# Output projection, first SwiGLU strips and down projection re-staged in a hybrid decoder layer (one core)

## The chip, the cores and the metric

The kernel runs on one core of a Trainium2 chip. The metric is device time in microseconds of one execution; lower is better. The core has five engines with instruction queues of their own: TensorE (PE in the rows; PEld is its weight load), VectorE (DVE), ScalarE (ACT), GpSimd (POOL) and SyncE (SP), which here issues the DMAs. Each engine takes its instructions strictly in order, so an instruction that waits holds up everything behind it on that engine.

## The reference, cut to what matters

One decoder layer on x of 1024 tokens by 1024 channels, in fp32. Three branches (gated linear attention, forgetting attention, cross-attention) are merged with gates; the change begins behind that:

```python
x = x + merged @ w_out[l]
h2 = _rmsnorm(x, g_ffn[l])          # x * rsqrt(mean(x*x)) * g
x = x + (jax.nn.silu(h2 @ w_ffn_gate[l]) * (h2 @ w_ffn_up[l])) @ w_ffn_down[l]
```

The hidden width of the SwiGLU is 2816.

## The kernel before

Channels lie on partitions, tokens in the free dimension: x1[j][h] is one 128x512 tile, channel block j (0 to 7) of token half h (0 or 1). Every fp32 matmul is done as three matmuls of rounded parts (mm3, L843, L845, L847: hi·hi, hi·lo, lo·hi). So each operand is split first: ScalarE casts it to the rounded high part (L903, tiles h or ...h), VectorE subtracts that from the raw tile to get the low part (L904, tiles l or ...l). A weight strip comes by DMA into a raw tile w4 (128x1024) and gives one h4 and one l4.

- **Merge** (to about 924 us of the span): the branches are summed into acc and split into mgh and mgl.
- **Output projection** (out_half, L919 to L932): for token half 0 and then 1, eight products of 24 matmuls, one per channel block j: load x (L919) and the weight strip wout (L921), split, multiply, add x to the result (L927), store the sum x_d (L928), square it (L930) and add the squares (L932).
- **Norm factors** (half_factors, L940 to L947): the squares are summed over partitions on TensorE, the inverse root comes from GpSimd (L108), and a product with a diagonal (L946) spreads it to all partitions as rbc (L947). The norm weight and the factor are then applied together in one VectorE instruction (L952, normed).
- **SwiGLU** (gate_up): 11 pairs of a gate strip and an up strip, 256 hidden channels each. A strip needs seven products of a Strassen-like scheme on sums of the token and channel halves (right operands B11, B21, T2, T1, T3, B22, T4; only B11 and B21 come from token half 0 alone). A product is 12 matmuls (four blocks of 128 channels by three), so a strip is seven products and a pair fourteen. What a product leaves in PSUM is kept by a ScalarE copy (L1031, tile t) or added to a kept tile by VectorE (L994). One PSUM bank goes on accumulating after its copy, so TensorE waits for that copy. The pair ends by storing act_d (L1073); then four loads of down weights go into cells d (L1076), are summed on VectorE and stored as sum_d (L1082).
- **Down projection** (down): four blocks of 3, 3, 3 and 2 pairs, which load act_d and sum_d back, split them and add into acc, in block 0 on top of the loaded x_d (L1136).

Tiles come from rotating pools: w4 has 5 buffers, h4 and l4 3 each, the cells (x1, acc, t, T, d) 16. TensorE's order is that of the program text. The order on the other engines and on SP is set at build time by a scheduler, which lets an instruction go ahead of others when the scheduler's own estimate says that its inputs are ready.

Of the kernel before, what the change touches and what calls it, by code (L numbers as in the profile page):

```python
# [12 lines left out]
F32 = mybir.dt.float32  # L13
# [64 lines left out]
def trunk(tc, xT, memT, wT, wmkv, wmq0, wmq1, wgv, wfox, a2, par, cst, wbr, wout, wfg, wfu, wfd, outT):  # L78
# [18 lines left out]
    identr = cp.tile([P, P], F32R, name="identr")  # L97
    negr = cp.tile([P, P], F32R, name="negr")
    mhalf = cp.tile([P, 1], F32, name="mhalf")
    hbg = cp.tile([P, 24], F32, name="hbg")  # L100
    gs = cp.tile([P, 6], F32, name="gs")
    rc = cp.tile([P, KT], F32, name="rc")
    rbc = cp.tile([P, S], F32, name="rbc")
# [26 lines left out]
    psA = pool(A, "psA", space=PSUM)  # L130
    bank = lambda tag, bufs: psA.tile([P, 512], F32, tag=tag, bufs=bufs, name=tag)
# [725 lines left out]
    cell = lambda name: ap_.tile([P, 512], F32, tag="cell", bufs=16, name=name)  # L857
# [5 lines left out]
    tp = pool(BM, "tg")  # L863
# [25 lines left out]
    merge_lane()  # L889
    Y.close()  # L890

# [4 lines left out]
    w4 = lambda: ws.tile([P, S], F32, tag="w4", bufs=5, name="w4")  # L896
# [3 lines left out]
    l2 = lambda: ws.tile([P, 512], F32R, tag="l2", bufs=2, name="l2")  # L900

# [9 lines left out]
    hops = {}  # L911

    def out_half(h):
# [3 lines left out]
        for j in range(KT):  # L917
            x1[j][h] = x = cell("x1")
            nc.sync.dma_start(x, xT[j][:, sl])  # L919
            raw = w4()  # L920
            nc.sync.dma_start(raw, wout[j])  # L921
            hi, lo = split(h4(), l4(), raw)
# [4 lines left out]
            nc.vector.tensor_tensor(x, x, ps, ALU.add)  # L927
# [3 lines left out]
            if j:  # L931
                nc.vector.tensor_tensor(ssq, ssq, sq, ALU.add)  # L932
            yield ssq

    def half_factors(h, ssq):
# [11 lines left out]
        nc.scalar.copy(rbc[:, H2[h]], ps)  # L947
        yield

    def normed(k, h):  # L950
        x = x1[k][h]
        nc.vector.scalar_tensor_tensor(x, x, pr[:, C_GFFN + k:C_GFFN + k + 1], rbc[:, H2[h]], ALU.mult, ALU.mult)  # L952
        return x
# [18 lines left out]

# [5 lines left out]
    def products(A, B, nk, reads):  # L978

        banks = {}  # L980
        for i, (bk, an, bn) in enumerate(SEQ):
            first = bk not in banks
            if first:
                banks[bk] = bank8()
            ps = banks[bk]
            for k in range(nk):
                (ah, al), (bh, bl) = A(an, k), B(bn, k)
                mm3([ps], ah, al, [(bh, bl)], first and k == 0, k == nk - 1, not first)
            reads[i](ps)
            yield  # L990

    BM.close()
    hp2 = pool(root, "h2b")
    add = lambda o, a, b: nc.vector.tensor_tensor(o, a, b, ALU.add)  # L994
    sub = lambda o, a, b: nc.vector.tensor_tensor(o, a, b, ALU.subtract)

    def weights(src):
# [6 lines left out]
        a = split(h4(), l4(), ra)  # L1004
# [18 lines left out]
    def gate_up(p):  # L1023

        g = [[None, None], [None, None]]
        u = [[None, None], [None, None]]

        def keep(t, i, l):
# [5 lines left out]
        def plus(t, i, l, then):  # L1034
# [5 lines left out]
        silu = lambda i, l: nc.scalar.activation(g[i][l], g[i][l], AF.Silu)  # L1040

        def silu_last(ps):
            g[1][0] = cell("t")
            nc.scalar.activation(g[1][0], ps, AF.Silu)

        mul = lambda i, l: nc.vector.tensor_tensor(u[i][l], u[i][l], g[i][l], ALU.mult)

        def mul_last(ps):
            u[1][0] = cell("t")
            nc.vector.tensor_tensor(u[1][0], ps, g[1][0], ALU.mult)  # L1050

        reads = lambda t, then, last: [keep(t, 0, 0), plus(t, 0, 0, then), keep(t, 0, 1), keep(t, 1, 1),
                                       plus(t, 1, 1, then), plus(t, 0, 1, then), last]
        wg = weights(wfg[p])
        gg_ = products(wg, hB, 4, reads(g, silu, silu_last))
        if p == 0:
            yield from (next(gg_) for i in range(2))
        else:
            yield from gg_
        wu = weights(wfu[p])  # L1060
        uu_ = products(wu, hB, 4, reads(u, mul, mul_last))
        if p == 0:
            yield from (next(uu_) for i in range(2))
            yield from gg_
        yield from uu_
        (b11, b12), (b21, b22) = u
        t1, t2, t3, t4 = (cell("T") for i in range(4))
        sub(t1, b12, b11)
        sub(t2, b22, t1)
        sub(t3, b22, b12)  # L1070
        sub(t4, b21, t2)
        for i, t in enumerate((b11, b21, t2, t1, t3, b22, t4)):
            nc.sync.dma_start(act_d[p][i], t)  # L1073
        a11, a12, a22, a21 = d = [cell("d") for i in range(4)]
# [8 lines left out]
        yield  # L1083

    run = gate_up(0)
    next(run)
    next(fac)
    next(run)
    next(run)
# [155 lines left out]
```

## Time and profile before

| | |
|---|---|
| median of 3 runs | 1755.86 us (1755.05 to 1757.85) |
| profiled execution | 1756.35 us, of which the span from first to last instruction is 1754.6 |
| TensorE busy | 1665.9 us (95%), mean granted clock 0.985 |
| VectorE, ScalarE, GpSimd busy | 989.3 (56%), 628.9 (36%), 103.1 us (6%) |
| DMA | 219.74 MB, 125 GB/s over the span |

A row of the timeline gives the start and the duration in us, the engine, the line in the kernel, the operation and its tiles, and in square brackets how long the engine stood idle before and what released it. "x4" is four instructions in a row. Clock is the share of TensorE's full rate (2.4 GHz) that was granted; half of it is 1.2 GHz.

### The profile page before, as it was taken

How to read it: one execution, taken by the hardware profiler on the slowest of the kernel's cores; microseconds unless marked ns; L12 is line 12 of the kernel's file. 1: busy time of each engine (PE TensorE's matmuls, PEld its weight loads, DVE VectorE, ACT ScalarE, POOL GpSimd, SP SyncE). 2: the span in 40 equal slices, each digit the busy share in tenths (PEclk: the TensorE clock that was granted, in tenths of full speed). 3: DMA queues.
4: the chain of work that ended last, by engine and by line, in shares of the span. 5: the costliest groups of instructions: out<-in, count | busy, mean ns of one | idle time of the engine just before them, and what ended most of it. 6: DMA issues, size and time to landing. Idle time of an engine off the chain costs nothing.

```text
span 1754.6 us, 21924 instructions
## 1 busy us (share of the span) xinstructions
PE 1665.9 (95%) x8411; PEld 1393.1 (79%) x8411; DVE 989.3 (56%) x1577; ACT 628.9 (36%) x1072; POOL 103.1 (6%) x88
## 2 busy tenths in 40 slices
PE   8999999999999999999998968999999999699999
PEld 6889988879799999988886856777777777577777
DVE  8435553452436555454474677565566665666766
ACT  6334553232224444342122324333332333433431
POOL 2000100000010100000450000000000000000000
PEclk9999999999999999999998988999999999899999
DMA  6431221111222211236555312454444445865654
GB/s 228 133 122 58 64 73 50 61 66 58 67 72 88 62 62 34 69 116 205 191 181 198 114 48 86 150 159 155 142 142 148 148 138 165 293 209 161 197 154 141
DMA packets 152297, 219.74 MB, mean 125 GB/s; under 512 B 11120, under 2 KB 93568, under 8 KB 152192
## 3 DMA queue, kind: packets, MB, share of 16 engines
q1 hardware_dynamic: 152192, 218.34, 38.3%
q8 instruction: 66, 1.08, 0.3%
q14 instruction: 39, 0.32, 0.1%
HBM read 159.25 MB, written 59.05 MB: 124 GB/s over the span
## 4 chain that ended last, share of the span: by engine, by line
PE 75%; DVE 9%; DMA 9%; SPq 3%; issue 2%; ACT 2%; POOL 0%; DVEq 0%; ACTq 0%
PE ps L843 11%; PE ps L845 11%; PE ps L847 11%; PE pt L156 4%; PE pt L158 4%; PE pt L157 4%; PE pm L235 4%; PE pm L236 4%; PE pm L237 4%; DMA d<-in_wfd 4%; PE pm L198 2%; DMA w<-act_d 2%; DVE l L904 2%; PE pm L202 2%; PE pm L200 2%
## 5 line engine op out<-in xcount | busy, mean ns | idle before, releaser
L843 PE MATMUL ps<-hbh,h 128*128 128x512 f32 x660 | 265.7, 403 | 66.3 <-ACT t L1031 35.2
L903 ACT CAST h<-w 128x1024 fp32r<-128x1024 f32 (+4 forms) x168 | 144.6, 861 | 368.5 <-PE ps L845 296.6
L845 PE MATMUL ps<-hbl,h 128*128 128x512 f32 x660 | 262.4, 398 | 0.0
L847 PE MATMUL ps<-hbh,l 128*128 128x512 f32 x660 | 262.3, 397 | 0.0
L904 DVE TENSOR_TENSOR l<-w,h 128x1024 fp32r<-128x1024 f32 (+4 forms) x168 | 166.0, 989 | 92.5 <-ACT h L903 92.4
L843 PEld LDWEIGHTS ps<-hbh,h 128*128 128x128 f32 x660 | 124.9, 189 | 108.3 <-ACT t L1031 39.8
L235 PE MATMUL pm<-whi,hh 128*128 128x384 f32 (+2 forms) x512 | 162.2, 317 | 0.0
L237 PE MATMUL pm<-whi,hl 128*128 128x384 f32 (+2 forms) x512 | 159.0, 310 | 0.0
L236 PE MATMUL pm<-wlo,hh 128*128 128x384 f32 (+2 forms) x512 | 158.9, 310 | 0.0
L847 PEld LDWEIGHTS ps<-hbh,l 128*128 128x128 f32 x660 | 124.8, 189 | 30.3
L845 PEld LDWEIGHTS ps<-hbl,h 128*128 128x128 f32 x660 | 125.0, 189 | 28.6
L156 PE MATMUL pt<-hh,whi 128*128 128x512 f32 x352 | 142.2, 404 | 0.0
L158 PE MATMUL pt<-hh,wlo 128*128 128x512 f32 x352 | 138.1, 392 | 0.0
L157 PE MATMUL pt<-hl,whi 128*128 128x512 f32 x352 | 138.1, 392 | 0.0
L994 DVE TENSOR_TENSOR acc<-ps,acc 128x512 f32<-128x512 f32 x112 | 76.8, 689 | 50.3 <-PE ps L847 47.6
L843 PE MATMUL ps<-hah,h 128*128 128x512 f32 x264 | 103.7, 393 | 0.9 <-ACT h L903 0.9
L847 PE MATMUL ps<-hah,l 128*128 128x512 f32 x264 | 103.2, 391 | 0.9 <-DVE l L904 0.8
L845 PE MATMUL ps<-hal,h 128*128 128x512 f32 x264 | 103.0, 390 | 0.0
L235 PEld LDWEIGHTS pm<-whi,hh 128*128 128x128 f32 x512 | 96.4, 188 | 2.6
L236 PEld LDWEIGHTS pm<-wlo,hh 128*128 128x128 f32 x512 | 96.4, 188 | 2.5
L237 PEld LDWEIGHTS pm<-whi,hl 128*128 128x128 f32 x512 | 96.3, 188 | 0.0
L188 DVE TENSOR_TENSOR wlo<-raw,whi 128x512 fp32r<-128x512 f32 (+2 forms) x64 | 48.3, 756 | 77.3 <-ACT whi L187 76.8
(301 smaller groups left out, 3065.5 us busy)
## 6 DMA issues: line engine op xcount, KB each, us to landing
w<-act_d SPq DMA_DIRECT2D x33, 512.0 KB, 4.1
tg<-tg_d SPq DMA_DIRECT2D x24, 512.0 KB, 3.5
raw<-in_wT SPq DMA_DIRECT2D x22, 512.0 KB, 4.1
tg_d<-gz SPq DMA_DIRECT2D x22, 512.0 KB, 2.9
w<-in_wfg SPq DMA_DIRECT2D x22, 512.0 KB, 4.4
w<-in_wfu SPq DMA_DIRECT2D x22, 512.0 KB, 3.7
act_d<-T SPq DMA_DIRECT2D x44, 256.0 KB, 6.0
d<-in_wfd SPq DMA_DIRECT2D x44, 256.0 KB, 6.2
```

Source lines behind the costliest of these rows:

```text
L156: nc.tensor.matmul(ps, hi[:, ks], hh[k][:, sl], start=k == 0, stop=False)
L157: nc.tensor.matmul(ps, hi[:, ks], hl[k][:, sl], start=False, stop=False)
L158: nc.tensor.matmul(ps, lo[:, ks], hh[k][:, sl], start=False, stop=k == KT - 1)
L235: nc.tensor.matmul(ps[:, :n], hh[k][:, ms], hi, start=k == 0, stop=False)
L236: nc.tensor.matmul(ps[:, :n], hh[k][:, ms], lo, start=False, stop=False)
L237: nc.tensor.matmul(ps[:, :n], hl[k][:, ms], hi, start=False, stop=k == KT - 1)
L843: nc.tensor.matmul(ps, hi, a, start=first, stop=False, skip_group_check=more)
L845: nc.tensor.matmul(ps, hi, b, start=False, stop=False, skip_group_check=more)
L847: nc.tensor.matmul(ps, lo, a, start=False, stop=last, skip_group_check=more)
L903: nc.scalar.copy(hi, raw)
L904: nc.vector.tensor_tensor(lo, raw, hi.bitcast(F32), ALU.subtract)
L994: add = lambda o, a, b: nc.vector.tensor_tensor(o, a, b, ALU.add)
```

## The change

- The first wout strip (j = 0 of half 0) is loaded and split under the branches, into buffers of its own (wout0).
- rbc, identr and three other constants move to pools that are freed; cells grow from 16 to 18, w4 from 5 to 6.
- In half 1 the norm weight is applied by ScalarE (L992 of the kernel after) as soon as a block is done, ahead of the factor, which is multiplied later; for blocks 4 to 7 the block j - 4 is subtracted as well. The factor for half 1 then is a plain VectorE product.
- The first strips wfg[0], wfu[0] and wfg[1] do their first two products (B11, B21: token half 0) before the factors of half 1 are needed; the raw first halves of the latter two strips are loaded early (early, e1, e2), their other parts are made later (lazy).
- The order of the sums behind the factor changes (T2 first), and the products of q0 and q1 alternate.
- down_sums uses w4 tiles in place of cells, and stands ahead of the products of its pair instead of behind them (pair 0's stands in pair 4).
- Down block 0 no longer loads x_d into acc: its first product of each tile is copied by ScalarE. x_d is added in block 1. The loads of the next block's act_d are called at jj = 2 of the block before.

```diff
-    rbc = cp.tile([P, S], F32, name="rbc")
-    cell = lambda name: ap_.tile([P, 512], F32, tag="cell", bufs=16, name=name)
+    cell = lambda name: ap_.tile([P, 512], F32, tag="cell", bufs=18, name=name)
     merge_lane()
+    wout0 = load_split(w0p, wout[0], S, "w0", 1, 1)
     Y.close()
-    w4 = lambda: ws.tile([P, S], F32, tag="w4", bufs=5, name="w4")
+    w4 = lambda: ws.tile([P, S], F32, tag="w4", bufs=6, name="w4")
...
-            raw = w4()
-            nc.sync.dma_start(raw, wout[j])
-            hi, lo = split(h4(), l4(), raw)
+            if h == j == 0:
+                hi, lo = wout0
+            else:
+                raw = w4()
+                nc.sync.dma_start(raw, wout[j])
+                hi, lo = split(h4(), l4(), raw)
...
-    halves = [out_half(h) for h in range(2)]
-    for ssq in halves[0]:
-        pass
-    fac = half_factors(0, ssq)
-    for j, ssq in enumerate(halves[1]):
-        if j in (0, 1):
+    fac = half_factors(ssq)
+    for j, ssq in enumerate(out_half(1)):
+        if j == 0:
             next(fac)
         if j == 1:
+            rb = next(fac)
             for k in range(KT):
-                hops["B11" if k < 4 else "B21", k % 4] = hop(hp1, "ha", 8, normed(k, 0))
-    fac = half_factors(1, ssq)
+                x = x1[k][0]
+                nc.vector.scalar_tensor_tensor(x, x, gain(k), rb, ALU.mult, ALU.mult)
+                hops["B11" if k < 4 else "B21", k % 4] = hop(hp1, "ha", 8, x)
+        x = x1[j][1]
+        nc.scalar.activation(x, x, AF.Copy, scale=gain(j))
+        if j > 3:
+            sub(x, x, x1[j - 4][1])
+    fac = half_factors(ssq)
...
-        a11, a12, a22, a21 = d = [cell("d") for i in range(4)]
+    def down_sums(p):
+
+        ta, tb = w4(), w4()
+        a11, a12, a22, a21 = d = [t[:, s] for t in (ta, tb) for s in H2]
...
+    wg0 = strips(wfg[0])
+    e1, e2 = early(wfu[0]), early(wfg[1])
+    q0, q1, q2 = pairs[0].gate(wg0), pairs[0].up(late("u0", wfu[0], e1)), pairs[1].gate(late("g1", wfg[1], e2))
+    go(q0, 4)
     next(fac)
-    next(run)
-    next(run)
-    next(fac)
+    go(q0, 4)
+    go(q1, 2)
+    rb = next(fac)
+    go(q1, 6)
+    go(q2, 8)
...
     for k in range(4):
-        (b11, b12), (b21, b22) = x1[k], x1[k + 4]
-        normed(k, 1)
-        normed(k + 4, 1)
-        t2 = w4()[:, :512]
-        sub(b11, b12, b11)
-        sub(t2, b22, b11)
+        t3, t2 = x1[k + 4][1], w4()[:, :512]
+        mul(t3, t3, rb)
+        add(t2, t3, x1[k][0])
         hops["T2", k] = hop(hp2, "hb", 20, t2)
-        sub(b21, b21, t2)
+        sub(x1[k + 4][0], x1[k + 4][0], t2)
+    lazy["u0"] = strips(wfu[0], e1)
...
+    for i in range(5):
+        go(q0, 4)
+        go(q1, 4)
+    pairs[0].store(0)
+    lazy["g1"] = strips(wfg[1], e2)
     for p in range(1, NP):
-        for _ in gate_up(p):
-            pass
+        q = q2 if p == 1 else Pair.gate(pair := Pair(), strips(wfg[p]))
+        if p == 1:
+            pair = pairs[1]
+        down_sums(p)
+        if p == 4:
+            down_sums(0)
+        go(q)
+        go(pair.up(strips(wfu[p])))
+        pair.store(p)
...
-            if p0 == 0:
-                for j in (jj, jj + 4):
-                    for h in range(2):
-                        acc[j][h] = cell("acc")
-                        nc.sync.dma_start(acc[j][h], x_d[j][h])
+            if jj == 2 and not last:
+                down_ops(p0 + n)
...
+                    if acc[j][h] is None:
+                        acc[j][h] = cell("acc")
+                        nc.scalar.copy(acc[j][h], ps)
+                        return
...
+            if b == 1:
+                for j in (j1, j2):
+                    x = w4()
+                    for h, s in enumerate(H2):
+                        nc.sync.dma_start(x[:, s], x_d[j][h])
+                        add(acc[j][h], acc[j][h], x[:, s])
```

Three places show what the scheduler made of it. **First place: half 1 of the output projection.** SP's queue before, around the load of the wout strip for block j = 2 (w4_8831):

```order
L928 DMA x_d3_0_8290<-x1_8435 128x512
L921 DMA w4_8793<-in_wout 128x1024
L928 DMA x_d4_0_8292<-x1_8473 128x512
L921 DMA w4_8831<-in_wout 128x1024
L928 DMA x_d5_0_8294<-x1_8511 128x512
L921 DMA w4_8869<-in_wout 128x1024
```

SP's queue after, around the same load (now w4_8770):

```order
L941 DMA x_d5_0_8308<-x1_8523 128x512
L941 DMA x_d6_0_8310<-x1_8561 128x512
L941 DMA x_d7_0_8312<-x1_8599 128x512
L941 DMA x_d0_1_8299<-x1_8638 128x512
L941 DMA x_d1_1_8301<-x1_8685 128x512
L934 DMA w4_8770<-in_wout 128x1024
L934 DMA w4_8809<-in_wout 128x1024
```

Before, that load stood five stores ahead of the store of block 1 of half 1; after, it stands behind it. On VectorE before, the low part of that strip (l4_8834) and the first two of the eight instructions that apply weight and factor to half 0:

```order
L927 TENSOR_TENSOR x1_8672<-x1_8672,ps_8680 128x512
L904 TENSOR_TENSOR l4_8834<-w4_8831,h4_8833 128x1024
L932 TENSOR_TENSOR ssq_8625<-ssq_8625,sq_8707 128x512
L952 SCALAR_TENSOR_TENSOR x1_8323<-x1_8323,pr_97,rbc_106 128x512
L952 SCALAR_TENSOR_TENSOR x1_8359<-x1_8359,pr_97,rbc_106 128x512
```

On VectorE after, the last three of those eight and the same low part (l4_8773):

```order
L989 SCALAR_TENSOR_TENSOR x1_8523<-x1_8523,pr_97,w4_8725 128x512
L989 SCALAR_TENSOR_TENSOR x1_8561<-x1_8561,pr_97,w4_8725 128x512
L989 SCALAR_TENSOR_TENSOR x1_8599<-x1_8599,pr_97,w4_8725 128x512
L913 TENSOR_TENSOR hal_8729<-x1_8337,hah_8728 128x512
L913 TENSOR_TENSOR hal_8734<-x1_8371,hah_8733 128x512
L913 TENSOR_TENSOR l4_8773<-w4_8770,h4_8772 128x1024
```

The low part has moved from ahead of all eight to behind them and two splits.

**Second place: a pair of the SwiGLU.** ScalarE before, from the last cast of a strip on (h2 and h4 are parts of the strips to come, t the kept products):

```order
L903 CAST h2_10396<-w4_10375 128x512
L903 CAST h4_10380<-w4_10374 128x1024
L1031 COPY t_10286<-ps_10273 128x512
L1040 ACTIVATE t_10286<-t_10286 128x512
L1031 COPY t_10315<-ps_10273 128x512
L903 CAST h4_10386<-w4_10376 128x1024
```

ScalarE after, at the same place:

```order
L912 CAST h2_10432<-w4_10411 128x512
L1054 COPY t_10322<-ps_10309 128x512
L912 CAST h4_10416<-w4_10410 128x1024
L1073 ACTIVATE t_10322<-t_10322 128x512
L1054 COPY t_10351<-ps_10309 128x512
L912 CAST h4_10422<-w4_10412 128x1024
```

The first kept copy (t) of the strip now stands ahead of the cast of the next strip's first part. SP's queue after holds, in one pair, the loads of down weights, the sums' stores and the next up strip in this order:

```order
L1098 DMA w4_9998<-in_wfd 128x4x128 x2
L1098 DMA w4_9999<-in_wfd 128x4x128 x2
L1022 DMA w4_10113<-in_wfu 128x1024
L1104 DMA sum_d3_8328<-w4_9999 128x4x128 x2
L1104 DMA sum_d3_8328<-w4_9998 128x4x128 x2
L1023 DMA w4_10114<-in_wfu 128x1024
```

Before, the sums lay in cells, and no load of a strip stood behind the wait of their stores in this way.

**Third place: behind the factor of half 1.** VectorE before, where the low part of the second piece of strip wfu[0] (l4_9065) stands among the first sums of the token halves:

```order
L952 SCALAR_TENSOR_TENSOR x1_8943<-x1_8943,pr_97,rbc_106 128x512
L995 TENSOR_TENSOR x1_8323<-x1_8626,x1_8323 128x512
L995 TENSOR_TENSOR x1_8359<-x1_8672,x1_8359 128x512
L904 TENSOR_TENSOR l4_9065<-w4_9054,h4_9064 128x1024
L995 TENSOR_TENSOR x1_8397<-x1_8753,x1_8397 128x512
```

VectorE after, where that piece (w4_9187) is made and split (l4_9194) behind the low parts of nearly all the token sums (hbl, 20 of them in all):

```order
L913 TENSOR_TENSOR hbl_9268<-x1_8485,hbh_9267 128x512
L913 TENSOR_TENSOR hbl_9272<-x1_8523,hbh_9271 128x512
L913 TENSOR_TENSOR hbl_9276<-x1_8561,hbh_9275 128x512
L908 TENSOR_TENSOR w4_9187<-w4_9187,w4_9185 128x512
L913 TENSOR_TENSOR hbl_9280<-x1_8599,hbh_9279 128x512
L908 TENSOR_TENSOR w4_9188<-w4_9185,w4_9187 128x512
L913 TENSOR_TENSOR l4_9194<-w4_9187,h4_9193 128x1024
```

It has moved from the head of the stretch to its end.

## Rows read from the trace of the kernel before

**Rows 1.** The page: busy time of TensorE; granted clock in 40 slices, in tenths.

```profile
PE 1665.9 (95%) x8411; PEld 1393.1 (79%) x8411; DVE 989.3 (56%) x1577; ACT 628.9 (36%) x1072; POOL 103.1 (6%) x88
PEclk9999999999999999999998988999999999899999
```

**Rows 2.** Waits of TensorE: line, releaser, us in total, times, longest.

```profile
PE ps L843 <- ACT t L1031: 35.2, 11, 21.3
PE ps L843 <- DVE acc L994: 21.6, 9, 14.1
PE ps L843 <- DVE t L994: 8.9, 10, 1.6
```

**Rows 3.** Timeline from merge to output projection (SP, ACT, DVE, PE).

```profile
923.32 3.12 SPq L921 DMA_DIRECT2D w<-in_wout  x5
929.43 1.04 ACT L903 CAST h<-w 128x1024 fp32r<-128x1024 f32 x1 [3.13 <-DMA w<-in_wout]
930.50 1.23 DVE L904 TENSOR_TENSOR l<-w,h 128x1024 fp32r<-128x1024 f32 x1 [3.10 <-ACT h L903]
930.52 0.79 PE L843 MATMUL ps<-mgh,h 128*128 128x512 f32 x1 [6.79 <-ACT h L903]
936.64 0.42 PE L845 MATMUL ps<-mgl,h 128*128 128x512 f32 x1
```

**Rows 4.** Windows: us, TensorE busy (matmuls), granted clock, DMA share, GB/s.

```profile
1061.39:1067.00 5.61, 5.61 (x14) 0.55 0.01 3
1527.67:1533.00 5.33, 5.33 (x17) 0.73 1.07 384
```

**Rows 5.** Timeline of half 1 of the output projection, behind block 1.

```profile
990.70 0.69 DVE L927 TENSOR_TENSOR x<-x,ps 128x512 f32<-128x512 f32 x1 [2.79 <-PE ps L847]
991.41 0.33 SPq L928 DMA_DIRECT2D x_d<-x  x1
993.33 5.39 DVE L952 SCALAR_TENSOR_TENSOR x<-x,pr,rbc 128x512 f32<-128x512 f32 x8
```

**Rows 6.** DMA issues: count, KB each, median us from issue to landing.

```profile
w<-in_wfu SPq DMA_DIRECT2D x22, 512.0 KB, 3.7
d<-in_wfd SPq DMA_DIRECT2D x44, 256.0 KB, 6.2
sum_d<-d SPq DMA_DIRECT2D x44, 256.0 KB, 2.6
w<-in_wout SPq DMA_DIRECT2D x16, 512.0 KB, 4.5
```

**Rows 7.** Timeline from the output projection to pair 0 (DVE, PE).

```profile
1025.15 0.69 DVE L927 TENSOR_TENSOR x<-x,ps 128x512 f32<-128x512 f32 x1 [1.59 <-PE ps L847]
1061.39 0.79 PE L843 MATMUL ps<-hbh,h 128*128 128x512 f32 x1 [21.25 <-ACT t L1031]
1066.55 0.39 PE L843 MATMUL ps<-hbh,h 128*128 128x512 f32 x1
1086.15 0.40 PE L843 MATMUL ps<-hbh,h 128*128 128x512 f32 x1
```

**Rows 8.** Timeline of one gate strip in the pairs (ACT, PE, DVE).

```profile
1097.18 1.04 ACT L903 CAST h<-w 128x1024 fp32r<-128x1024 f32 x1 [4.85 <-PE ps L845]
1098.13 0.58 ACT L1031 COPY t<-ps 128x512 f32<-128x512 f32 x1
1098.77 0.50 PE L843 MATMUL ps<-hbh,h 128*128 128x512 f32 x1 [1.39 <-ACT t L1031]
1105.30 0.69 DVE L994 TENSOR_TENSOR d<-d 128x512 f32<-128x512 f32 x1 [3.80 <-DMA d<-in_wfd]
1111.04 0.50 PE L843 MATMUL ps<-hbh,h 128*128 128x512 f32 x1 [0.81 <-DVE t L994]
```

**Rows 9.** Timeline at the start of the down projection (DVE, PE).

```profile
1526.22 0.69 DVE L994 TENSOR_TENSOR d<-d 128x512 f32<-128x512 f32 x1 [4.98 <-DMA d<-in_wfd]
1527.67 0.76 PE L843 MATMUL ps<-hbh,h 128*128 128x512 f32 x1 [14.14 <-DVE acc L994]
```

More of the change, by code (lines that the diff above doesn't have):

```diff
@@ L911, in trunk @@
     hops = {}
+    gain = lambda k: pr[:, C_GFFN + k:C_GFFN + k + 1]
     def out_half(h):
@@ L1003, in weights @@
         s2, s1, s3, s4 = sa[:, lo_], sa[:, hi_], sb[:, lo_], sb[:, hi_]
-        a = split(h4(), l4(), ra)
+        a = first or split(h4(), l4(), ra)
         add(s1, rb_[:, lo_], rb_[:, hi_])
@@ L1054, in gate_up @@
[L1054 to L1073, printed above, removed]
-        a11, a12, a22, a21 = d = [cell("d") for i in range(4)]
+        def reads(self, t, then, last):
+            return [self.keep(t, 0, 0), self.plus(t, 0, 0, then), self.keep(t, 0, 1), self.keep(t, 1, 1),
+                    self.plus(t, 1, 1, then), self.plus(t, 0, 1, then), last]
@@ new lines, in gate, with last, up @@
+        def gate(self, w):
+            g = self.g
+            def last(ps):
+                g[1][0] = cell("t")
+                nc.scalar.activation(g[1][0], ps, AF.Silu)
+            return products(w, hB, 4, self.reads(g, lambda i, l: nc.scalar.activation(g[i][l], g[i][l], AF.Silu), last))
+        def up(self, w):
+            g, u = self.g, self.u
+            def last(ps):
+                u[1][0] = cell("t")
+                mul(u[1][0], ps, g[1][0])
+            return products(w, hB, 4, self.reads(u, lambda i, l: mul(u[i][l], u[i][l], g[i][l]), last))
@@ new lines, in store @@
+        def store(self, p):
+            (b11, b12), (b21, b22) = self.u
+            t1, t2, t3, t4 = (cell("T") for i in range(4))
+            sub(t1, b12, b11)
+            sub(t2, b22, t1)
+            sub(t3, b22, b12)
+            sub(t4, b21, t2)
+            for i, t in enumerate((b11, b21, t2, t1, t3, b22, t4)):
+                nc.sync.dma_start(act_d[p][i], t)
+    def down_sums(p):
+        ta, tb = w4(), w4()
+        a11, a12, a22, a21 = d = [t[:, s] for t in (ta, tb) for s in H2]
@@ L1137, in down @@
+    def down(b, p0, n):
+        first, last = b == 0, p0 + n == NP
+        for q in range(n):
+            if (ORDER[0], p0 + q) not in ops:
+                down_ops(p0 + q)
+        for jj in range(4):
+            if jj == 2 and not last:
+                down_ops(p0 + n)
             three = lambda t: t[:, :n * 2 * P].rearrange("p (n c) -> p n c", c=2 * P)
@@ L1167, in down @@
                      into(j1, 1, True), into(j2, 0, True)]
-            for _ in products(get, lambda name, k: ops[name, k], n, reads):
-                pass
+            if b == 1:
[4 more added lines that the diff above has]
+                        add(acc[j][h], acc[j][h], x[:, s])
+            go(products(get, lambda name, k: ops[name, p0 + k], n, reads))
     p0 = 0
-    for n in DOWN:
-        down(p0, n, p0 + n == NP)
+    for b, n in enumerate(DOWN):
+        down(b, p0, n)
         p0 += n
```

122 lines of the change are left out of this document (67 added, 55 removed).

## The prediction

> **What bounds the kernel now.** I read the page's busy shares first, then TensorE's waits, then the timeline around each of them. TensorE is busy 95% of the span and at full clock in nearly all slices [rows 1]. So little can be won but its idle time, and since its products are the same before and after, the change is worth what it takes away or adds in gaps and in half-rate matmuls (1.2 GHz granted instead of 2.4) behind gaps. Behind the merge the waits fall into five places [rows 2, 3]: 6.79 us for the first output weight strip; 21.25 us ahead of the first T2 product; ten gaps of about 1.4 us for a ScalarE copy and ten of 0.6 to 1.6 us for a VectorE addition, one of each in every later pair; 14.14 us at the start of the down projection; and 7.5 us in eight further waits of the down projection (21.6 less 14.1). A full-rate product of 12 matmuls takes 2.80 us: seven of them lie between 1066.55 and 1086.15 [rows 7]. The profiled execution took 1756.35 us, 0.5 above the median of the three runs; I work from it and take off the 0.5 at the end.
>
> **1. First output strip: -8.3.** Before, SP issues the wout loads at 923.32, the cast of the first runs at 929.43, and TensorE idles from 923.73 to 930.52 [rows 3]. It then runs at half rate: 14 matmuls start between 930.52 and 936.64, in 6.12 us where 14 x 0.233 = 3.27 would do, a loss of 2.85. After, strip 0 is split long before, and 24 matmuls (5.6 us) run from about 923.7 to 929.3. Strip 1 is then the late one: released by the same merge, it can be issued no earlier than 923.32, so its cast ends where the first cast ended, at 930.5. That leaves a gap of 1.2 to 1.8. So 6.79 + 2.85 - 1.3 = 8.3 goes. The load and split of strip 0 lie under the branches, where TensorE does not wait for them; its cover there is one cast and one subtraction of 1.04 and 1.23 us, which is the worst that it costs.
>
> **2. A new wait in half 1 of the output projection: +11.** Before, the wout strip of block 2 is loaded well ahead. After, its load is behind the store of block 1, which waits for that block's product. Call the end of that product X (990.70 before) [rows 5]. The store is issued at X + 0.71, the load behind it at about X + 1.0; it lands 4.5 later [rows 6] at X + 5.5, and its cast ends at X + 6.6. VectorE is late too: the eight scale instructions start at X + 2.6 and take 5.39 [rows 5], two splits of about 0.67 follow, and only then the low part, 1.23, which ends near X + 10.3. TensorE has the spread of the factor to do until about X + 0.9 (half of the 2.2 that both factor products take, below), then waits to X + 6.6, does the two matmuls that need no low part, and waits to X + 10.3: 5.7 + 2.8 = 8.5 idle. Half rate behind it costs about what it did behind the 6.79 (2.5 to 2.85). The gap is hidden only if the load were issued a product earlier, which the order does not allow. Lower bound: without VectorE's part 5.7 and no loss of clock, +6; upper: landing as the slowest load of the rows [rows 6], 6.2 in place of 4.5, +13. I take +11, the step by step value. The other things that half 1 gets (eight gain instructions on ScalarE of the length of a copy, four subtractions, two early splits) lie beside products of 5.6 us each and cost nothing unless ScalarE falls behind; each gain waits for a store, but what stands behind it is needed one product later.
>
> **3. Transition to the pairs: -3.** From the last addition of the output projection (1025.15) to the end of the twelfth product it takes 61.0 us before [rows 7]: four products on half 0, the 21.25 us in which VectorE scales and sums the tokens, then eight products, the first at half rate (clock 0.55 in that window [rows 4]). After, six products come first, so TensorE is free at 19.0: six of 2.80 and 2.2 for the factor's own products (before, the 15.0 us from 1025.15 to 1040.14, where the idle time begins, held four products and those, so they are under 3.8). VectorE begins its sums at about 10 and comes to the first low part of T2 behind 8 products, 4 sums and 10 other instructions of about 0.67 (14.5): T2 of q0 can go at 24.5, a gap of 5.6. T2 of q1 needs the second piece of wfu[0], whose subtraction stands behind some 23 token sums and splits: 24.5 + 23 x 0.68 gives about 40, its cast 1.04 and low part 1.23 about 42.6, a second gap of 13. Half rate behind it, then the remaining products: twelve are done at about 58. So -3. Bounds: the second gap no longer than the first, -10; the two together as long as the old one and 4 longer for a second half-rate stretch, +4.
>
> **4. Ten pairs: -20.** The ScalarE gap: a cast that had waited 4.85 us for TensorE stands ahead of the kept copy, so the copy starts 0.95 late and TensorE 1.39 [rows 8]. After, the copy stands first: 13.9 us of the 35.2 [rows 2] go. The VectorE gap: VectorE sits 3.80 us on a load of down weights, and the addition that TensorE needs comes late by 0.81 [rows 8]. After, those loads are issued a strip ahead of their sums (19.6 us, seven products) so they have landed. But the next up strip's second load is now behind the sums' stores, and the sum of that strip stands on VectorE ahead of an addition that TensorE needs. I get it issued about 5 us into the up strip, landed (3.7 [rows 6]) at 9, and the addition of the fifth product (ends at 14.0) on time with some 1.3 us to spare before TensorE needs it at 16.8. I keep 2.8 us of the 22.8 for pairs in which that margin fails, as in pair 4 with two sets of sums. Bounds: nothing left, -22.8; both VectorE waits late like the old one, -5.
>
> The Trainium skill, "DMA: Bandwidth & Descriptors", Anatomy of one DMA, prices a DMA at 2.0 us and its bytes over 436 GB/s, and its section Issuing engines are not separate DMA queues says that all queues share the same 16 engines; by that, an estimate, a strip takes 3.2 us and the four loads of down weights together 4.4. The 3.7 agrees within half a microsecond, the 6.2 does not: the rows have such loads among seven stores of activations. By the page the margin holds in every pair and the sum would be 2.8 us lower; by the 6.2 some pairs fail, which is why I keep the 2.8.
>
> **5. Start of the down projection: -10.7.** VectorE sits 4.98 us on down weights and only then does the addition that TensorE waits for, 14.14 us in all [rows 9]; half rate follows (5.33 us at clock 0.73, a loss of 1.4 [rows 4]). After, no sums of weights are left here, and x_d is not loaded. Late next are the low part of the first strip (about 1.7) and ScalarE's copy into acc, which stands behind two casts that wait for loads (about 3.1): -15.5 + 4.8. Bounds: both hidden, -15.5; a landing of 6.2 in each, -6.
>
> **6. Rest of the down projection: +2.** The eight waits of 7.5 us partly stay. New are 16 additions of x in block 1, each on a fresh load in VectorE's queue ahead of additions that TensorE waits for; 0.69 us each is hidden, a landing is not always. A wait of 3.80 on VectorE made a gap of 0.81 [rows 8], four groups of them up to 2 each: from -3 (some of the 7.5 goes with the earlier loads) to +8.
>
> Sum: -8.3 + 11 - 3 - 20 - 10.7 + 2 = -29.0; 1756.35 - 29.0 - 0.5 = 1726.9, so 1727.
>
> **Rivals.** (a) The new waits are short: +6 in place of +11 in half 1, -10 in the transition, the pairs clean at -22.8, the down start at -12, the rest 0: -47, so 1709. For it: my delays are chains of instructions, and the margins on TensorE's side were counted with none to spare. Against: the load behind the store is in the order itself.
> (b) The pair gap moves: the old VectorE gap (8.9 in ten) stays in the up strip, and a second of the same size comes where the strip's sum waits for its late load: pairs -5, total -14, so 1742. For it: VectorE sat on such loads before; against: they are issued a strip earlier.
> (c) Slower: the chain in the up strip becomes the bound of a pair. Loads of down weights (6.2), four sums (2.8), four store issues of 0.33, the load (3.7), four sums and a split (4.0), the addition (0.7) are 18.7 us; if the first of these starts 2 us into the up strip, not in the gate strip, the addition ends at 20.7 where 16.8 is wanted: about 4 us in each of ten pairs, 40 against the 22.8 saved. The other terms are -9.0, so +8.2 in all: 1764. It is slower from about 3.5 us a pair. For it: w4 tiles must be free before these loads start, where cells were free before; against: the tiles come free in the gate strip by the order.
> (d) The ScalarE copy is not what the 1.39 us hang on and they stay: -29 + 13.9, so 1741. Against: copy and matmul follow each other within 0.06 us [rows 8].
>
> **Chances.** Forecast 0.62 (own range 1717 to 1737); (a) 0.12; (b) and (d) together 0.15; a mixture of (b) and longer new waits that eats the gain 0.05; (c) 0.06. Less than 0.2%, 3.5 us, can't be told from no change here. Faster then is 0.62 + 0.12 + 0.15 = 0.89, within 0.2% 0.05, slower 0.06. The range to hold the time 8 times in 10 runs from (a) to just beyond (b): 1709 to 1744.
>
> **What would show it.** Step 1: no idle time of 6.8 us at the first output matmul, one of 1 to 2 us at the second product. Step 2: a gap of 5 to 6 us and one of 2 to 4 us at block 2 of half 1, for a cast that waits for wout and for a low part, and a lower clock behind. Step 3: two gaps ahead of T2 products, the second on a low part of wfu. Step 4: pairs of 39.3 to 39.6 us, no gap on a kept copy. Step 5: no gap above 4 us at the first down products. I am wrong if the pairs keep regular gaps of over 1 us, or if half 1 has none.

## The result and the profile after

The changed kernel takes 1728.47 us (median of four runs, 1727.31 to 1730.37) beside 1756.86 us for the kernel before on the same chip: ratio 0.9841, 95% interval 0.9823 to 0.9858. That is 28.4 us faster, where 1727 had been forecast. The profiled execution has a span of 1726.7 us, 27.9 less than before (1754.6).

The page after, answering to [rows 1]: the same 8411 matmuls, now 97% of the span.

```profile
PE 1672.0 (97%) x8411; PEld 1401.4 (81%) x8411; DVE 992.7 (57%) x1581; ACT 643.4 (37%) x1096; POOL 101.6 (6%) x88
PEclk9999999999999999999999997999999999999999
```

TensorE's waits from 900 us on, answering to [rows 2] (line, releaser, us in total, times, longest). No single wait of 21.3 or 14.1 us is left, and the ten waits for ScalarE's copy (`t`) are gone; what leads now is a cast.

```profile
PE ps L844 <- ACT h L912: 17.6, 3, 12.2
PE ps L844 <- DVE acc L907: 5.4, 5, 2.2
PE ps L844 <- DVE t L907: 4.6, 3, 2.1
PE ps L846 <- DVE hbl L913: 4.3, 1, 4.3
PE ps L844 <- ACT acc L1214: 4.3, 1, 4.3
PE ps L848 <- DVE l L913: 4.2, 3, 2.6
```

TensorE's timeline (start, us, engine, line, operation, in brackets the idle time before it and its releaser): the places that the prediction named, in order of time.

```profile
930.03 0.50 PE L848 MATMUL ps<-mgh,l 128*128 128x512 f32 x1 [0.53 <-DVE l L913]
987.15 0.80 PE L844 MATMUL ps<-mgh,h 128*128 128x512 f32 x1 [5.18 <-ACT h L912]
990.93 0.80 PE L848 MATMUL ps<-mgh,l 128*128 128x512 f32 x1 [2.55 <-DVE l L913]
1051.26 0.79 PE L846 MATMUL ps<-hbl,h 128*128 128x512 f32 x1 [4.32 <-DVE hbl L913]
1067.98 0.79 PE L844 MATMUL ps<-hbh,h 128*128 128x512 f32 x1 [12.19 <-ACT h L912]
1167.13 0.50 PE L844 MATMUL ps<-hbh,h 128*128 128x512 f32 x1 [1.93 <-DVE t L907]
1497.03 0.79 PE L844 MATMUL ps<-hbh,h 128*128 128x512 f32 x1 [4.26 <-ACT acc L1214]
```

The 6.79 us of [rows 3] have become 0.53; 5.18 and 2.55 are new, in half 1; 21.25 [rows 7] has become 4.32 and 12.19; 14.14 [rows 9] has become 4.26. Cut at the same points of the work in both traces, the 27.9 us lie so (us; "out" is the output projection from the end of the merge to its last addition):

| stretch | before | after | difference | forecast |
|---|---|---|---|---|
| out | 101.42 | 104.27 | +2.85 | -8.3 + 11 |
| to the start of the 13th strip product | 61.00 | 57.06 | -3.9 | -3 |
| to the first down matmul | 422.91 | 402.89 | -20.0 | -20 |
| to the third down product | 18.61 | 9.97 | -8.6 | -10.7, with the clock behind it |
| to the last matmul | 222.85 | 225.60 | +2.75 | +2 |

The rest is 0.9 us by which the merge ends earlier, which no step had. One execution is not exact to this: in the second profile of the changed kernel (below), with the same span of 1726.7 us, the five stretches take 103.24, 58.20, 400.18, 10.05 and 225.56 us, and the merge ends 1.6 us later than before. So agreement closer than 3 us in a single stretch is partly luck.

### The profile page after: what moved, and what is told of

Its sections match the earlier page's. It is cut to its first block, busy times and chain, and to the rows that moved or that the text cites. A ratio compares the mean times of both kernels' runs of the same rounds, so it can differ in the third digit from the quotient of the medians.

```text
span 1726.7 us, 21934 instructions
## 1 busy us (share of the span) xinstructions
PE 1672.0 (97%) x8411; PEld 1401.4 (81%) x8411; DVE 992.7 (57%) x1581; ACT 643.4 (37%) x1096; POOL 101.6 (6%) x88
## 4 chain that ended last, share of the span: by engine, by line
PE 85%; DVE 6%; DMA 5%; ACT 2%; issue 1%; SPq 0%; POOL 0%; DVEq 0%; ACTq 0%
PE ps L844 14%; PE ps L848 14%; PE ps L846 14%; PE pt L157 5%; PE pt L159 4%; PE pt L158 4%; PE pm L236 4%; PE pm L238 4%; PE pm L237 4%; PE pm L199 2%; PE pm L203 2%; PE pm L201 2%; DMA w<-in_wfd 2%; DVE hbl L913 1%; DMA w<-in_wfu 1%
## 5 line engine op out<-in xcount | busy, mean ns | idle before, releaser
L844 PE MATMUL ps<-hbh,h 128*128 128x512 f32 x660 | 265.5, 402 | 29.9 <-ACT h L912 12.2
L848 PE MATMUL ps<-hbh,l 128*128 128x512 f32 x660 | 266.1, 403 | 0.0
L913 DVE TENSOR_TENSOR l<-w,h 128x1024 fp32r<-128x1024 f32 (+4 forms) x165 | 162.1, 985 | 60.5 <-ACT h L912 60.2
L848 PE MATMUL ps<-hah,l 128*128 128x512 f32 x248 | 96.7, 390 | 1.1 <-DVE l L913 1.1
L846 PE MATMUL ps<-hal,h 128*128 128x512 f32 x248 | 97.1, 392 | 0.0
L844 PE MATMUL ps<-hah,h 128*128 128x512 f32 x248 | 97.0, 391 | 0.0
L907 DVE TENSOR_TENSOR acc<-ps,acc 128x512 f32<-128x512 f32 x96 | 66.2, 690 | 46.0 <-PE ps L848 44.7
```

What stands on the lines that cost most here:

```text
L844: nc.tensor.matmul(ps, hi, a, start=first, stop=False, skip_group_check=more)
L846: nc.tensor.matmul(ps, hi, b, start=False, stop=False, skip_group_check=more)
L848: nc.tensor.matmul(ps, lo, a, start=False, stop=last, skip_group_check=more)
L913: nc.vector.tensor_tensor(lo, raw, hi.bitcast(F32), ALU.subtract)
```

## The experiments

Each is the changed kernel with one edit, unless it says otherwise. The changed kernel ran twice in this study, with medians 1728.47 and 1728.61; differences below are of medians against 1728.5, ratios against the kernel before on the same chip. That kernel's median was 1752.4 to 1756.9 in the four sets of runs, so a few us between sets are not to be read.

**No early first strip.**

```diff
-    wout0 = load_split(w0p, wout[0], S, "w0", 1, 1)
...
-            if h == j == 0:
-                hi, lo = wout0
-            else:
...
```

> The kernel after, but without the early load and split of the first output strip. Theory (the strip's wait was the whole gap): the gap ahead of the first output matmul comes back with its 6.8 us and the half-rate matmuls behind it, about 2.9, less the 0.8 that the kernel after still waits there: +8.9 us against the kernel after, 1737. Rival (the early load is paid for under the branches, or the merge end moves with it): under +5 us.

1735.80 us, ratio 0.9889 (0.9874 to 0.9903): +7.3. The old wait is back, with matmuls of 0.79 us behind it (TensorE's timeline):

```profile
931.14 0.79 PE L844 MATMUL ps<-mgh,h 128*128 128x512 f32 x1 [5.74 <-ACT h L911]
```

So the early strip is worth 7.3 us by the medians, 5.4 to 8.4 by the two ratios, and the wait in half 1 is not its consequence: it is there without it, with 5.06 and 2.67 us.

**Output weights of half 1 written ahead.**

```diff
+    AHEAD = 3
...
+            for jn in range(j, min(KT, j + 1 + AHEAD * h)):
+                if jn not in raws and not h == jn == 0:
+                    raws[jn] = w4()
+                    nc.sync.dma_start(raws[jn], wout[jn])
...
```

> The kernel after, but in half 1 of the output projection the loads of the output strips are written up to three blocks ahead, so that those of blocks 2 and 3 stand ahead of the store of block 1 in SP's queue. Theory (the load behind the store is what opens the gaps of 5.18 and 2.55 us at block 2, and they lower the clock): both go, with about 2.9 us of half rate: -10 to -11 us, 1718. Rival (VectorE's eight scale instructions are the real limit, the load only comes first): the gap of 5.18 goes and one of 2 to 4 us at a low part remains, -4 to -6 us.

1716.39, ratio 0.9783 (0.9765 to 0.9802): -12.1. No gap of 0.4 us or more is left between 932 and 1036, and the output projection ("out" in the table) takes 93.12 us. VectorE in that run does the same eight scalings, but the low part `l` of the next strip now stands ahead of them:

```profile
983.95 1.23 DVE L913 TENSOR_TENSOR l<-w,h 128x1024 fp32r<-128x1024 f32 x1 [0.16 <-ACT h L912]
...
985.70 5.39 DVE L994 SCALAR_TENSOR_TENSOR x<-x,pr,w 128x512 f32<-128x512 f32 x8
```

Both halves of the wait hung on one load's place in SyncE's queue.

**First up strip's weight sums ahead of the T2 terms.**

```diff
+    lazy["u0"] = strips(wfu[0], e1)
     for k in range(4):
...
-    lazy["u0"] = strips(wfu[0], e1)
```

> The kernel after, but the other parts of wfu[0] are made ahead of the token sums behind the factor, not behind T2. Theory (VectorE's order sets both gaps ahead of the T2 products): the second gap, 12.2 us, goes with about 1.7 us of half rate; the first, 4.3, grows by the four sums and two splits that now stand ahead, about 4.2: -8 to -10 us, 1719. Rival (VectorE's total of work up to the last low part is the bound, the order only says where the wait shows): within 3 us of the kernel after.

1717.38, ratio 0.9789 (0.9773 to 0.9805): -11.1. The 12.19 us are gone; the waits ahead of them are 2.10 and 4.80 in place of 0.58 and 4.32, and 0.77 follows.

**16 slots in place of 18** (`bufs=18` to `bufs=16` in `cell`).

> The kernel after with 16 cells in place of 18. The order on ScalarE in the pairs stays as it is, with the kept copies ahead of the casts; copies wait for older stores of activations. Theory (the order, not the number of cells, frees the pairs): the pairs lose under 3 us; the kept copies of the first products must wait for the first token sums to leave their cells, so the first T2 product starts 3 to 6 us later, of which the second gap swallows most: 0 to +5 us in all. Rival (the cells do it): the ScalarE gaps of 1.4 us in ten pairs come back, and with them a wait as long as the 21 us ahead of T2: +15 us or more.

1727.21, ratio 0.9844 (0.9828 to 0.9860): -1.3, no difference. The two waits of the transition trade length (9.04 and 8.21). With the down sums out of the slots, 16 are enough.

**Down sums back in slots.**

```diff
-        ta, tb = w4(), w4()
-        a11, a12, a22, a21 = d = [t[:, s] for t in (ta, tb) for s in H2]
+        a11, a12, a22, a21 = d = [cell("d") for i in range(4)]
```

> Like the changed kernel, but the sums of the down weights use activation slots (cells) again as before, at the changed kernel's place in the program. With that the copy of a strip's first kept half stands behind the weight cast on ScalarE again, and the loads of the down weights stand among stores that wait for sums. My theory (the stretch of the ten strip pairs lost its 20 us because the copy runs ahead of the cast, and because the sums left the slots that the activations hold): about 1746 us, +14 to +23 against the changed kernel, with TensorE's gaps behind ScalarE (7 to 14 us summed over the pairs) back, and some of those behind VectorE. Rival (the slots of the sums don't matter, only where down_sums stands): under +3 us, about 1728.

1740.47, ratio 0.9931 (0.9916 to 0.9946): +12.0; the profiled span is 10.9 longer. From the last output addition to the first down matmul it takes 474.65 us in place of 459.95. ScalarE's timeline in one of the pairs:

```profile
1177.20 1.04 ACT L912 CAST h<-w 128x1024 fp32r<-128x1024 f32 x1 [4.87 <-DMA act_d<-T]
1178.15 0.58 ACT L1054 COPY t<-ps 128x512 f32<-128x512 f32 x1
```

And TensorE's waits in that run:

```profile
PE ps L844 <- ACT t L1054: 14.0, 10, 1.4
PE ps L844 <- DVE t L907: 2.1, 2, 1.9
```

The cast stands ahead of the copy again, as in [rows 8], and ten waits of 1.4 us are back. This strip begins at 1171.75, so its first copy runs 6.4 us into it. In the changed kernel (a strip that begins at 1128.87) the first copy runs 2.9 us into the strip, ahead of the cast:

```profile
1131.81 0.59 ACT L1054 COPY t<-ps 128x512 f32<-128x512 f32 x1 [2.36 <-PE ps L848]
1134.31 1.05 ACT L912 CAST h<-w 128x1024 fp32r<-128x1024 f32 x1 [1.91 <-PE ps L846]
```

My theory holds for ScalarE. It fails for VectorE: its waits didn't come back, and the time is at or just under the lower end of what I expected (12.8 to 15.8 by the two ratios).

**Down sums behind the store of the pair** (the call moved from ahead of `go(q)` to behind `pair.store(p)`).

> Like the changed kernel, but down_sums is called behind the store of the pair instead of ahead of it; its buffers stay those of the changed kernel. The copy of the first kept half stays ahead of the cast on ScalarE, but the strip loads stand behind the sums' stores in SyncE's order and VectorE waits for the down weights inside the gate strip. My theory (the order of SyncE's queue and of VectorE around the sums makes the gaps behind VectorE): +9 to +20 us, about 1740, with TensorE's gaps behind VectorE in the pairs back at 1 to 4 us each and none behind ScalarE. Rival (with the sums out of the slots their place is free): under +3 us.

1724.01, ratio 0.9838 (0.9822 to 0.9854): -4.5 by the medians, -0.5 to -3.5 by the two ratios. My theory falls: the old place makes nothing slower. One wait of over 0.4 us is left in the pairs, 0.83; the waits at 1167.13, 1210.03 and 1288.82 of the changed kernel are gone. SyncE in the two kernels shows why. In the changed kernel, the load of the second part of the next up strip (L1023) stands behind the sums' stores. Here is the up strip that begins at 1148.35 and holds the wait at 1167.13; VectorE waits for that load, then sums the strip, and only then does the addition that TensorE waits for:

```profile
1149.68 0.34 SPq L1022 DMA_DIRECT2D w<-in_wfu  x1
1154.33 2.58 SPq L1104 DMA_DIRECT2D sum_d<-w  x4
1158.56 0.34 SPq L1023 DMA_DIRECT2D w<-in_wfu  x1
1162.72 0.69 DVE L907 TENSOR_TENSOR w<-w 128x512 f32<-128x512 f32 x1 [3.77 <-DMA w<-in_wfu]
```

With the sums behind the store, in the same up strip (it begins at 1150.41), that load is issued 0.1 us into the strip instead of 10.2:

```profile
1144.26 0.35 SPq L1022 DMA_DIRECT2D w<-in_wfu  x1
1150.54 0.33 SPq L1023 DMA_DIRECT2D w<-in_wfu  x1
```

Nor does VectorE wait much for the down weights here: 3.9 us between 1090 and 1490, against 24.1 in the changed kernel.

**Norm weight not applied ahead.**

```diff
-        nc.scalar.activation(x, x, AF.Copy, scale=gain(j))
-        if j > 3:
-            sub(x, x, x1[j - 4][1])
...
-        mul(t3, t3, rb)
+        nc.vector.scalar_tensor_tensor(t3, t3, gain(k + 4), rb, ALU.mult, ALU.mult)
+        nc.vector.scalar_tensor_tensor(x1[k][1], x1[k][1], gain(k), rb, ALU.mult, ALU.mult)
+        sub(t3, t3, x1[k][1])
...
-        mul(b12, b12, rb)
```

> Like the changed kernel, but the norm weight is not applied ahead of the factor: no ScalarE scaling and no early differences in the second out projection; weight and factor are applied together on VectorE behind the factor, and the four differences come after it. My theory (this part is worth the first waits of the transition alone, four more VectorE operations of about 0.7 us behind the factor): 0 to +4 us, about 1730, with the wait at the start of the first strip longer by about 3 us and the 12 us wait behind the cast shorter or the same. Rival (the eight scalings and the early differences cost more in the out projection than they give): -2 us.

1729.93, ratio 0.9870 (0.9853 to 0.9886): +1.4 by the medians, +2 to +5 by the two ratios, 1.4 in the span. As expected in size; the first wait stays at 4.28, though, and is followed by one of 1.28, then 9.41 and 3.66 in place of 12.19. This part of the change is worth a few us at most.

**Residual loaded into the accumulators as before.**

```diff
+            if b == 0:
+                for j in (jj, jj + 4):
+                    for h in range(2):
+                        acc[j][h] = cell("acc")
+                        nc.sync.dma_start(acc[j][h], x_d[j][h])
...
-            if b == 1:
-                for j in (j1, j2):
...
```

> Like the changed kernel, but the residual is loaded into the accumulators in the first block of the down product again as before, instead of being added from a separate buffer in the second block. My theory (the start of the down product is set by the order of the weight casts and the first accumulator copies on ScalarE, not by these loads): within 3 us of the changed kernel, 1725 to 1731. The gap of 4.3 us behind the first accumulator copy would go if adds into a loaded accumulator, which stand on VectorE, take the copy's place: then -2 to -4 us. Rival (these loads were what delayed the start of the down product before): +5 to +8 us, about 1735.

1730.36, ratio 0.9873 (0.9858 to 0.9888): +1.9 by the medians, 2.6 to 5.6 by the two ratios, 3.2 in the span. What I said of the gap was wrong: it grows from 4.26 to 10.55 us. SyncE's first load of x into acc, that load's time to landing (smallest, median, largest of this one), and the addition on VectorE:

```profile
1495.84 0.67 SPq L1191 DMA_DIRECT2D acc<-x_d  x1
...
DMA to landing us min/median/max: 7.4/7.4/7.4
...
1503.21 1.42 DVE L907 TENSOR_TENSOR acc<-ps,acc 128x512 f32<-128x512 f32 x2
```

The load lands at 1503.2, when the addition starts. VectorE is busy until then with the low parts of other late loads, so this run doesn't tell which of the two held the addition. In the kernel before it is the same: the first load of x is issued at 1521.04 and lands 5.8 us later, and the addition starts at 1526.83.

Part of it is given back: from the third product to the end it takes 221.74 us in place of 225.60, for there are no additions of x. So the copy into acc gains 6.3 in the wait at the start, and the additions of x cost 3.9 later (3.5 of it in block 1, where they stand). The rival had the right place, and half of its price.

**The changed kernel again.**

> The changed kernel itself, on the same chip as the next three, as their base: the ratio found with the result, 0.984, within 0.002. The runs with the sums behind the store and with the sums in slots are to be read against this base; if its ratio is nearer 0.981, the first gained nothing and the scaled-ahead part is worth 5 us more than thought.

1728.61, ratio 0.9858 (0.9843 to 0.9873), the profiled span 1726.7 again. In the pairs TensorE's waits behind VectorE sum to 1.9 us here (1.49 and 0.36), against 4.6 in the first profile.

**Down sums in slots and behind the store, both as before.**

> Like the changed kernel, but the sums of the down weights use activation slots and stand behind the store of the pair, both as before the change. With slots but at the new place 14 us came back at ScalarE's copy and none at VectorE; with the old place but separate buffers nothing came back. My theory now (buffers and place each suffice to remove the VectorE gap, only the buffers remove the ScalarE gap): both gaps are back, ten of about 1.4 and ten of 0.6 to 1.6, +16 to +23 us against the changed kernel, about 1747. Rival (the VectorE gap went with the order of the strips' sums in the new program text, not with these two): the ScalarE gap alone, +11 to +15, about 1741.

1743.88, ratio 0.9945 (0.9933 to 0.9958): +15.3. The sum misleads; the waits decide for the rival:

```profile
PE ps L844 <- ACT t L1054: 12.5, 9, 1.4
PE ps L844 <- ACT acc L1213: 11.3, 2, 10.8
PE ps L844 <- DVE t L907: 1.4, 1, 1.4
```

ScalarE's waits are back, VectorE's ten are not (8.9 us in [rows 2], 1.4 here), and the start of the down product waits 10.8 us, since the copy into acc stands on ScalarE behind casts that wait 3.64 us for a load of down weights and 2.20 for one of act_d.

**Three moves together** (output weights ahead, up strip early, sums behind the store).

> The changed kernel with three moves of code: output weights of the second half written up to three blocks ahead (-10.9 alone), the first up strip's weight sums ahead of the T2 terms (-9.9 alone), the down weight sums behind the store of the pair (0 to -4 alone). My theory (the three waits lie in different stretches, so the gains add): -21 to -25 against the changed kernel, about 1705, with no gap over 5 us before the pairs and none over 1 us in them. Rival (the stretches are coupled by SyncE's queue, which issues all loads in order, so that part comes back in the pairs or at the start of the down product): -14 to -18, about 1712.

1703.81, ratio 0.9716 (0.9699 to 0.9734): -24.7. The gains add. One sign fails: a wait of 2.42 us is left in pair 1.

**The same, with the A22 load of each down strip ahead of the loads of sums.**

```diff
+            raw = one(w4())
+            nc.sync.dma_start(raw, wfd[jj, p0:p0 + n, :, 2, :].rearrange("n p c -> p n c"))
             for w in range(2):
                 for q in range(n):
                     nc.sync.dma_start(raws[1 + w][:, q, :] ...
```

> As the kernel with the three moves, but the small load of down weights of each strip (A22) is issued ahead of the loads of the sums instead of behind them. My theory (the 4.3 us gap at the start of the down product is the accumulator copy standing on ScalarE behind casts that wait for loads, this one's the last): -1 to -3 us against the three moves, with that gap at 2 to 3 us. Rival (the other loads that the casts wait for come as much later): 0, the gap as long behind a cast that waits for a sum.

1702.41, ratio 0.9709 (0.9696 to 0.9723): the best version, 52 us below the kernel before on that chip, and 1.4 below the three moves, which the intervals don't separate. The 4.44 us became three waits, 4.53 in sum, so neither theory had it. TensorE's timeline:

```profile
1471.18 0.50 PE L844 MATMUL ps<-hbh,h 128*128 128x512 f32 x1 [2.37 <-ACT acc L1219]
1477.33 0.50 PE L844 MATMUL ps<-hbh,h 128*128 128x512 f32 x1 [1.69 <-ACT acc L1219]
1480.16 0.49 PE L844 MATMUL ps<-hbh,h 128*128 128x512 f32 x1 [0.47 <-ACT acc L1219]
```

A window behind the first of them (span, then busy time of TensorE, weight loads, VectorE, ScalarE and GpSimd, the granted clock, DMA share, GB/s):

```profile
1471.18:1477.00 5.82, 4.46 (x18) 3.29 (x18) 4.59 (x8) 2.49 (x5) 0.00 (x0) 1.00 0.95 316
```

The clock is full: split waits cost only themselves here.

## Why the prediction was right, step by step

**1, first strip.** Right. What is left is 0.28 and 0.53 us where 1.3 was left in the estimate; taking the step out costs 7.3. With the wait in half 1 gone as well, the output projection takes 93.12 us, 8.3 less than before. One slip in the sum: the 14 starts enclose 13 intervals, so the half rate had cost 3.1 and not 2.85.

**2, half 1.** Right, and nearly so in its parts. The store at X + 0.7, the load right behind it, the cast, the eight scalings ahead of the low part (X is 981.16 here):

```profile
981.87 0.32 SPq L941 DMA_DIRECT2D x_d<-x  x1
982.28 6.64 SPq L934 DMA_DIRECT2D w<-in_wout  x6
...
983.15 5.38 DVE L989 SCALAR_TENSOR_TENSOR x<-x,pr,w 128x512 f32<-128x512 f32 x8
...
986.06 1.04 ACT L912 CAST h<-w 128x1024 fp32r<-128x1024 f32 x1 [0.22 <-DMA w<-in_wout]
...
989.65 1.22 DVE L913 TENSOR_TENSOR l<-w,h 128x1024 fp32r<-128x1024 f32 x1
```

In this timeline of SyncE, VectorE and ScalarE the load is issued 0.4 us behind the store, and the low part waits behind the scalings. TensorE goes on at X + 6.0 and X + 9.8, forecast X + 6.6 and X + 10.3. Idle 7.7, and 16 matmuls take 7.30 us of busy time at half clock (first window below, the clock third from the end of the row) where 16 x 0.233 = 3.7 would do: 11.3 in all, forecast 11 (8.5 idle and 2.5 at half rate). Written ahead, 12.1 comes back, 11.2 of it in this stretch.

```profile
987.15:997.00 9.85, 7.30 (x16) 5.31 (x17) 9.61 (x14) 4.96 (x8) 0.00 (x0) 0.50 0.80 298
1497.03:1503.00 5.97, 5.97 (x16) 4.73 (x17) 3.26 (x6) 2.87 (x5) 0.00 (x0) 0.57 1.03 381
```

**3, transition.** Right: gaps of 4.9 and 12.2 for 5.6 and 13, -3.9 for -3. The second hung on the strip's sums behind the token sums, as said, though TensorE waited there for the cast and not for the low part: ScalarE had waited 5.39 us for the sum on VectorE. Moved ahead, 11 us go.

**4, pairs.** The size is right (-20.0 in this profile, -22.7 in the second), the reason only in its first half. ScalarE's half is shown: with the cast ahead of the copy its waits return, which also ends rival (d). The pairs from 4 on take 38.98 to 39.80 us, close to the 39.3 to 39.6 named, pairs 2 and 3 42.72 and 41.35. The waits account for 18.2 of the 20.0: 22.8 gone, 4.6 new. The new ones are what I had kept 2.8 for, and the late second load is their cause. I had it issued about 5 us into the up strip. In this profile, in the quiet pairs from 4 on, it is issued 7.7 to 8.3 us into it; where it is issued 8.6 us into it, TensorE waits 0.55, and at 9.9 and 10.2 us 2.11 and 1.93.

VectorE's half is not as I gave it. The loads of down weights are not issued a strip (19.6 us) ahead of their sums, and VectorE goes on waiting for them. In pair 2 the last of them are issued at 1147.90, 5.7 us ahead. VectorE's waits for these loads between 1090 and 1490 us, before, after, and with place and buffers of the sums as before (us in total, times, longest):

```profile
DVE d L994 <- DMA d<-in_wfd: 41.3, 10, 6.7
DVE w L907 <- DMA w<-in_wfd: 24.1, 10, 3.9
DVE d L907 <- DMA d<-in_wfd: 23.5, 10, 5.2
```

With place and buffers as before, TensorE's waits still stay away, so it is neither of these two, alone or together. What differs on VectorE is what stands between its wait and the addition that TensorE needs. Before, two sums of a strip (`w`) stand there in nine of ten pairs, and the addition comes 5.0 us behind the wait:

```profile
1146.80 0.69 DVE L994 TENSOR_TENSOR d<-d 128x512 f32<-128x512 f32 x1 [3.73 <-DMA d<-in_wfd]
...
1150.60 1.28 DVE L995 TENSOR_TENSOR w<-w,w 128x512 f32<-128x512 f32 x2
1151.80 1.28 DVE L994 TENSOR_TENSOR t<-ps,t 128x512 f32<-128x512 f32 x2
```

With place and buffers as before, these two sums stand ahead of the wait, and here VectorE is ready before TensorE's product is:

```profile
1182.12 0.69 DVE L907 TENSOR_TENSOR d<-d 128x512 f32<-128x512 f32 x1 [1.97 <-DMA d<-in_wfd]
...
1186.40 0.69 DVE L907 TENSOR_TENSOR t<-ps,t 128x512 f32<-128x512 f32 x1 [0.28 <-PE ps L848]
```

In the changed kernel the addition comes 2.8 us behind nine of these ten waits. So a shorter wait and another order on VectorE took the place of the cause I gave; that the size came out is in this half luck. What brought them about is not shown. A sixth `w4` buffer, 18 slots and the order of the program text around the first pairs still differ from the kernel before; of these only 16 slots were tried, and with the sums out of them, where VectorE's ten waits stayed away too. Rivals (b) and (c) didn't come: no pair has a second wait.

The median landing of the 256 KB wfd loads went from 6.2 [rows 6] to 3.3 us. The Trainium skill, "DMA: Bandwidth & Descriptors", Anatomy of one DMA, has its fit for DMAs that GpSimd issues, and these are issued by SyncE; taken over all the same, it gives 2.6 us for one such load, an estimate. The trace after is 0.7 above it, the one before, where these loads stand among the activation stores, 3.6.

**5, start of the down product.** The step that was mis-sized: -10.7 forecast, -8.6 measured up to the matmul behind the wait, and the clock that I had taken off came on top. I had the late copy into acc at 3.1 us and full clock behind it. It waited 4.26, behind a cast that itself waited 2.57 for a load, and the window above shows clock 0.57: 16 matmuls in 5.97 us where 3.73 would do, 2.2 lost where before it was 1.4. So the term is -8.6 + 0.8 = -7.8, and the sign "no gap above 4 us" failed:

```profile
1495.98 0.51 ACT L912 CAST h<-w 128x384 fp32r<-128x384 f32 x1 [2.57 <-DMA w<-in_wfd]
1496.40 0.58 ACT L1214 COPY acc<-ps 128x512 f32<-128x512 f32 x1
```

The reading of [rows 9] was also short of one cause. Before, the first load of x landed as the addition started (see the run with the residual), so the sums of down weights were not alone in holding it. The change took both away, so the forecast did not suffer.

**6, rest of the down product.** +2.75, of which 0.8 is that clock: 1.95 for a forecast of 2. By blocks it is -0.9, +4.2, +0.2 and -0.7, and the +4.2 lies in block 1, which adds x, as said. The run with the residual in the accumulators puts the additions of x at 3.9.

Rival (a), 1709, needed a short wait in half 1 and a clean transition; only the three moves of code together got there.

## What to carry to other kernels

Where all loads and stores share one in-order queue, price a moved step by what is now queued behind a store that waits for a result; four lines that write such loads earlier gave 12 us here. Ask of each in-order engine which instruction that waits stands ahead of one that TensorE waits for: the same copy cost 1.4 us in ten pairs behind a cast and nothing ahead of it, while the number of slots made no difference. Where a wait goes, price its successor with the half rate that can stand behind it: at the start of the down product one wait of 4.44 us was followed by a clock of 0.50 over the next 5.5 us, three of 4.53 in sum by full clock. That is one run each, and a single short wait is no guarantee (next section). Where a wait goes away, look whether the engine that caused it still waits: here VectorE did, 24.1 us in the pairs, and what had changed was its order behind the wait.

## What the runs showed of the hardware

The half clock does not follow from the length of the wait just before it alone: behind 2.37 us the granted clock was 1.00, behind 1.93 us in the changed kernel 0.66 over the next 5 us (first row below), behind 2.42 us in the run with three moves 0.68 (second row), behind 4.26 us 0.57. The wait of 4.26 us cost a further 2.2 in slow matmuls, and those of 5.18 and 2.55 a further 3.6.

```profile
1167.13:1172.13 5.00, 5.00 (x15) 3.96 (x16) 3.44 (x5) 0.58 (x1) 0.00 (x0) 0.66 0.65 204
1092.95:1098.00 5.05, 5.05 (x15) 4.01 (x16) 2.41 (x4) 2.77 (x5) 0.00 (x0) 0.68 0.49 169
```
